# Loads cut in halves, and single row copies issued earlier, in a rank-ordered row scatter

## Chip, cores and metric

The kernel runs on one core of one Trainium2 chip. The metric is the device time of one execution in microseconds (us), as the median over several runs. The record gives every run in this document the state "fast" (granted TensorE clock 0.51 to 0.59). "Span" is the time from first to last instruction; in the recorded runs it is 1.7 to 2.0 us shorter than the device time. Every ratio compares a kernel with runs of the kernel before from the same rounds.

## The reference

Each of 8 batches has 2048 rows of 2560 float32 (10 KB a row). Row i goes to the place that its score takes in the sorted order of its batch:

```python
x = randn(8, 2048, 2560); scores = randn(8, 2048)
ranks = argsort(argsort(scores, axis=1), axis=1)
out[b, ranks[b, i], :] = x[b, i, :]
```

168 MB are read and 168 MB are written; the arithmetic is only the ranking.

## The kernel before

VectorE counts, for each score, how many scores of its batch are smaller. Rows then travel in two ways. All of them are moved by DMAs. The profile counts 16 DMA engines, which the queues share: from 200 to 240 us the packets of the three queues take 94.0, 4.2 and 4.2% of the time of 16 engines, 102% together. q0 is GpSimd's queue, q1 is SP's (SyncE) and q10 is ACT's (ScalarE). What was handed to a queue and has not yet passed is called its ring here; SP's and ACT's held up to 36 rows each. The trace records packets. A row copy is 16 packets of 640 B and 16 of 4 B (12,672 of each for ACT's 792 rows); loads and scatters come to 144 packets each (25,920 for 180 DMAs on q0), 128 of data (of 4 B for the 56 thin rows, which the scatters leave out) and 16 small ones. The small packets, 16 to a DMA, are called completion packets here.

The bulk of the rows goes through on-chip memory. GpSimd loads a block of 256 rows (2.6 MB, two rows to a partition) into one of 8 buffers and scatters it with two indirect DMAs of 128 rows each. It loads four blocks ahead, and a buffer is loaded again when its scatters have landed. The first 8 loads are made as two DMAs of 10 KB a partition, the other 50 as one of 20 KB:

```python
NBUF = 8; LAG = 4
BULK = [(b, g) for b in range(B) for g in range(len(GROUPS)) if g or b not in DIRECT]   # 58 blocks
HALVED = range(8)

def load(line, k, sem):
    ...
    for j in range(m if k in HALVED else 1):
        part = slice(j * D, (j + 1) * D) if k in HALVED else slice(0, m * D)
        line.eng.dma_start(out=xb[k % NBUF][:, part], in_=rows[:, part]).then_inc(sem, 16)
...
for k, (b, g) in enumerate(BULK):
    if k >= LAG and k + NBUF - LAG < len(BULK):
        scatters_done(pl, k - LAG)
        load_ahead(k + NBUF - LAG)
    pl.wait(*loaded[k])
    pl.after(dve, t_bulk[b, g])
    for j in range(GROUPS[g][1]):
        scatter(k, j)
nc.gpsimd.drain()
```

The other rows are copied one by one inside DRAM, by SP and ACT on queues of their own. The first block of batches 0 to 5 is copied in a hardware loop (128 rows on each of the two engines per batch), and seven further sets of 8 rows ("thin" rows) in straight-line code:

```python
todo = list(enumerate(THIN))                 # THIN = [(b, 4) for b in 1..7]
for b in DIRECT:                             # batches 0..5
    while todo and todo[0][1][0] < b:
        n, where = todo.pop(0)
        thin_rows(n, *where)                 # 8 rows, on SP or ACT in turn
    for h, (line, name) in enumerate(((sp, ENG.SP), (act, ENG.Activation))):
        line.after(dve, t_rows[b])
        with line.eng.Fori(0, half // G) as q:      # 16 rows a turn
            ...
for n, where in todo:
    thin_rows(n, *where)
for line in (sp, act):
    line.wait(s_rows[line], 16 * n_rows[line])
...
for k in range(max(0, len(BULK) - NBUF), len(BULK)):
    scatters_done(sp, k)
```

At the end SP waits for its row copies and for the last scatters. In the program the row wait stands first, but in the traces SP's step for it comes after the scatter waits (778.3 against 769.9 us in the kernel before).

Of the kernel before, what the change touches and what calls it, by code (L numbers as in the profile page):

```python
# [40 lines left out]
def kernel(  # L41
# [15 lines left out]
    DIRECT = range(6)  # L57
# [9 lines left out]
    THIN = [(b, 4) for b in range(1, B)]  # L67
    HOLES = range(48, 48 + 4)

    HALVED = range(8)  # L70

    STEPS = [(0, 1), (1, 2), (2, 4), (4, 8)]

# [28 lines left out]
    with tc.tile_critical(no_gpsimd_drain=True):  # L102
# [17 lines left out]
        def load(line, k, sem):  # L120
            b, g = BULK[k]
            r, m = GROUPS[g]
            rows = x[b, r:r + P * m, :].rearrange("(p j) d -> p (j d)", j=m)
            for j in range(m if k in HALVED else 1):
                part = slice(j * D, (j + 1) * D) if k in HALVED else slice(0, m * D)
                line.eng.dma_start(  # L126
                    out=xb[k % NBUF][:, part], in_=rows[:, part]
                ).then_inc(sem, 16)
                if k:
                    n_load[k % NBUF] += 1  # L130
# [3 lines left out]
        load(sp, 0, s_first)  # L134
        loaded = {0: (s_first, 16 * (2 if 0 in HALVED else 1))}

# [224 lines left out]
        def thin_rows(n, b, g):  # L361
            line, name = ((sp, ENG.SP), (act, ENG.Activation))[n % 2]
            r, m = GROUPS[g]
            line.after(dve, t_rows[b, g])
            _, at = nc.values_load_multi_w_load_instructions(
                thin_i[b, g][:],
                engines=[name],
                min_val=b * N * ROW,
                max_val=(b * N + N - 1) * ROW,
                skip_runtime_bounds_check_because=(  # L370
                    "a rank counts other scores of one batch of N, so it lies in 0..N-1"
                ),
            )
            for i in range(4 * m):
                row = b * N + r + HOLES[i % 4] * m + i // 4
                line.eng.dma_start(
                    out=out_bytes[bass.ds(at[i], ROW)],
                    in_=x_bytes[bass.ds(row * ROW, ROW)],
                ).then_inc(s_rows[line], 16)
                n_rows[line] += 1  # L380

        todo = list(enumerate(THIN))
        for b in DIRECT:
            while todo and todo[0][1][0] < b:
                n, where = todo.pop(0)
                thin_rows(n, *where)
            for h, (line, name) in enumerate(((sp, ENG.SP), (act, ENG.Activation))):
                line.after(dve, t_rows[b])
                half = WIDE // 2
                with line.eng.Fori(0, half // G) as q:  # L390
                    _, at = nc.values_load_multi_w_load_instructions(
                        rows_i[b][:, bass.ds(half * h + q * G, G)],
                        engines=[name],
                        min_val=b * N * ROW,
                        max_val=(b * N + N - 1) * ROW,
                        skip_runtime_bounds_check_because=(
                            "a rank counts other scores of one batch of N, so it lies in 0..N-1"
                        ),
                    )
                    for i in range(G):  # L400
                        row = b * N + GROUPS[0][0] + half * h + i
                        line.eng.dma_start(
                            out=out_bytes[bass.ds(at[i], ROW)],
                            in_=x_bytes[bass.ds(q * (G * ROW) + row * ROW, ROW)],
                        ).then_inc(s_rows[line], 16)
                n_rows[line] += half
# [73 lines left out]
```

## Time and profile before

| | before |
|---|---|
| device time | 782.2 us (782.14 to 783.19) |
| span of the profiled run (its device time 781.49 us) | 779.7 us |
| bulk: packets on q0 (data and completion) | 25,920 |
| row copies: SP (q1), ACT (q10) | 800 and 792 rows |
| last packet of q0 / of SP's rows / of ACT's rows | 769.4 / 775.4 / 773.3 us |

The prediction below shows the lines of this profile. In the slices of the span, a digit is the busy share of one fortieth of the span in tenths. In the DMA view, a queue has its packets, its megabytes and its share of the time of 16 engines. In the list of waits, an entry has the total, the number of times and the longest, in us. The last packets come from the trace's record of each DMA packet, which has start, duration, queue and size but not the engine.

### The profile page before, as it was taken

How to read it: one execution, taken by the hardware profiler on the slowest of the kernel's cores; microseconds unless marked ns; L12 is line 12 of the kernel's file. 1: busy time of each engine (PE TensorE's matmuls, PEld its weight loads, DVE VectorE, ACT ScalarE, POOL GpSimd, SP SyncE). 2: the span in 40 equal slices, each digit the busy share in tenths (PEclk: the TensorE clock that was granted, in tenths of full speed). 3: DMA queues.
4: the chain of work that ended last, by engine and by line, in shares of the span. 5: the costliest groups of instructions: out<-in, count | busy, mean ns of one | idle time of the engine just before them, and what ended most of it. 6: DMA issues, size and time to landing. Idle time of an engine off the chain costs nothing.

```text
span 779.7 us, 8177 instructions
## 1 busy us (share of the span) xinstructions
PE 35.4 (5%) x170; PEld 30.5 (4%) x170; DVE 399.8 (51%) x825; ACT 0.0 (0%) x1; POOL 150.2 (19%) x189
## 2 busy tenths in 40 slices
PE   4000020020020020120000000000000000000000
PEld 4000010010010010120000000000000000000000
DVE  5999979979979979899999200000000000000000
ACT  0000000000000000000000000000000000000000
POOL 4113122212121211112121212121212121220100
PEclk9999995555555555565555555555555555555555
DMA  8999999999999999999999999999999999999995
GB/s 360 418 419 419 426 415 425 415 421 416 424 418 424 416 421 417 425 417 423 419 421 420 422 419 421 420 422 422 417 425 416 426 416 425 417 424 418 419 415 101
DMA packets 77186, 320.15 MB, mean 411 GB/s; under 512 B 28448, under 2 KB 53920, under 8 KB 53920
## 3 DMA queue, kind: packets, MB, share of 16 engines
q0 software_dynamic: 25920, 300.90, 90.7%
q1 hardware_dynamic: 25904, 10.93, 5.5%
q10 hardware_dynamic: 25344, 8.16, 4.5%
q14 instruction: 17, 0.14, 0.0%
q8 instruction: 1, 0.02, 0.0%
HBM read 168.41 MB, written 168.35 MB: 432 GB/s over the span
## 4 chain that ended last, share of the span: by engine, by line
DMA 49%; another core or an unknown queue 19%; DVE 13%; POOL 7%; issue 6%; PE 1%; POOLq 0%; SPq 0%
DMA out_dram<-x,rank_i 43%; DVE trash L238 12%; DMA x<-in_x_dram 6%; POOL out_dram L422 5%; POOL x L126 1%; PE ps_all L196 0%; DVE s_all L339 0%; DMA s_in<-in_scores_dram 0%; PE ps_col L175 0%; POOLq L446 0%; DVE rank_i L276 0%; DVE rank L270 0%; DVE rank L264 0%; PE ps_row L298 0%
## 5 line engine op out<-in xcount | busy, mean ns | idle before, releaser
L238 DVE TENSOR_SCALAR_CACHE_REDUCE trash<-s_all,s_col 128x1792 bf16<-128x1792 f32 (+7 forms) x240 | 315.2, 1348 | 4.6
L422 POOL DMA_INDIRECT out_dram<-x,rank_i x116 | 112.7, 972 | 141.8 <-DMA x<-in_x_dram 36.4
L126 POOL DMA_DIRECT2D x<-in_x_dram x64 | 35.7, 560 | 445.7 <-DMA out_dram<-x,rank_i 426.6
L238 DVE SCALAR_TENSOR_TENSOR trash<-s_all,s_col,mask 128x256 bf16<-128x256 f32 x128 | 61.6, 481 | 0.0
L196 PE MATMUL ps_all<-ident,s_col 128*128 128x128 f32 x128 | 28.5, 416 | 3.1 <-DVE s_all L339 2.8
L196 PEld LDWEIGHTS ps_all<-ident,s_col 128*128 128x128 f32 x128 | 26.8, 226 | 4.2 <-DVE s_all L339 3.2
L298 PE MATMUL ps_row<-ident,rank 128*1 128x128 f32 x26 | 7.0, 366 | 392.5 <-DVE rank_i L284 335.2
L339 DVE COPY s_all<-ps_all 128x512 f32<-128x512 f32 x32 | 20.2, 685 | 1.7 <-PE ps_all L196 1.4
L238 DVE DVE_READ_ACCUMULATOR trash<-s_all,s_col 128x1 f32 x240 | 19.9, 83 | 0.0
L298 PEld LDWEIGHTS ps_row<-ident,rank 128*1 128x1 f32 x26 | 1.9, 95 | 395.8 <-DVE rank_i L284 337.6
L238 DVE DVE_READ_ACCUMULATOR trash<-s_all,s_col,mask 128x1 f32 x128 | 10.6, 83 | 0.0
L309 DVE TENSOR_SCALAR thin_i<-ps_row 1x8 int32<-1x8 f32 x7 | 1.1, 154 | 17.7 <-PE ps_row L298 17.7
L324 DVE TENSOR_SCALAR rows_i<-ps_row 1x256 int32<-1x256 f32 x6 | 2.5, 412 | 4.1 <-PE ps_row L298 4.1
L183 DVE COPY s_col<-ps_col 128x128 f32<-128x128 f32 x1 | 0.3, 290 | 4.5 <-PE ps_col L175 4.5
L175 PE MATMUL ps_col<-ident,s_in 8*128 8x8 f32 x16 | 2.1, 262 | 3.6 <-DMA s_in<-in_scores_dram 3.6
L175 PEld LDWEIGHTS ps_col<-ident,s_in 8*128 8x128 f32 x16 | 2.0, 211 | 3.6 <-DMA s_in<-in_scores_dram 3.6
L276 DVE CAST rank_i<-rank 128x16 int32<-128x16 f32 (+3 forms) x11 | 1.9, 173 | 0.4
L270 DVE TENSOR_TENSOR rank<-rank,acc 128x16 f32<-128x16 f32 (+3 forms) x11 | 1.9, 170 | 0.4
L264 DVE TENSOR_TENSOR rank<-acc,acc 128x16 f32<-128x16 f32 (+3 forms) x11 | 1.9, 170 | 0.4
L284 DVE TENSOR_SCALAR rank_i<-rank,hole 128x2 int32<-128x2 f32 x7 | 1.6, 228 | 0.2
L156 POOL TENSOR_SCALAR_AFFINE_SELECT mask<-mask 128x256 f32<-128x256 f32 x2 | 0.8, 398 | 0.0
L168 DVE MEMSET acc<- 128x128 f32 x1 | 0.2, 165 | 1.1 <-SPq L102 1.1
(10 smaller groups left out, 1.8 us busy)
## 6 DMA issues: line engine op xcount, KB each, us to landing
x<-in_x_dram POOLq DMA_DIRECT2D x50, 2560.0 KB
x<-in_x_dram POOLq DMA_DIRECT2D x14, 1280.0 KB
out_dram<-in_x_dram SPq DMA_DIRECT2D x800, 10.0 KB
out_dram<-in_x_dram ACTq DMA_DIRECT2D x792, 10.0 KB
x<-in_x_dram SPq DMA_DIRECT2D x2, 1280.0 KB, 9.3
out_dram<-x,rank_i POOLq DMA_INDIRECT x116, 48.4
s_in<-in_scores_dram SPq DMA_DIRECT2D x1, 64.0 KB
```

Source lines behind the costliest of these rows:

```text
L126: line.eng.dma_start(out=xb[k % NBUF][:, part], in_=rows[:, part]).then_inc(sem, 16)
L175: nc.tensor.transpose(out=ps_col[:, B * c:B * (c + 1)], in_=s_in[:, r + j:r + m * P:m], identity=ident[:B, :B],)
L196: nc.tensor.transpose(out=ps_all[:, P * c:P * (c + 1)], in_=s_col[:, c, b:b + 1].to_broadcast([P, P]), identity=ident[:],)
L238: do(out=trash[i][:, :P * (hi_c - lo_c)], in0=s_all[:, P * lo_c:P * hi_c], accum_out=acc[i][:, col:col + 1], **how,)
L264: nc.vector.tensor_tensor(out=rank[:, cols], in0=acc[0][:, cols], in1=acc[1][:, cols], op=OP.add)
L270: nc.vector.tensor_tensor(out=rank[:, cols], in0=rank[:, cols], in1=acc[2][:, cols], op=OP.add)
L276: nc.vector.tensor_copy(out=rank_i[:, cols], in_=rank[:, cols])
L284: nc.vector.tensor_scalar(out=rank_i[:, cols], in0=rank[:, cols], scalar1=hole[:], scalar2=None, op0=OP.add,)
L298: nc.tensor.transpose(out=ps_row[:1, P * j:P * (j + 1)], in_=rank[:, col:col + 1], identity=ident[:],)
L324: nc.vector.tensor_scalar(out=rows_i[b][:].rearrange("o (p j) -> o p j", p=P), in0=ps_row[:1, :WIDE].rearrange("o (j p) -> o p j", p=P), s ...
L339: nc.vector.tensor_copy(out=s_all[:, 512 * q:512 * (q + 1)], in_=ps_all[:, 512 * q:512 * (q + 1)],)
L422: nc.gpsimd.indirect_dma_start(out=out_flat, out_offset=bass.IndirectOffsetOnAxis(ap=rank_i[:, col:col + 1], axis=0), in_=xb[k % NBUF][:, ...
```

## The change

Two things are altered: 12 more loads are issued as halves, and the thin rows of batches 5 to 7 are issued ahead of the last loop in place of after it. The intent is to let the row copies keep pace, so that they don't end after everything else.

```diff
-    HALVED = range(8)
+    HALVED = range(20)
@@
-            while todo and todo[0][1][0] < b:
+            while todo and (todo[0][1][0] < b or b == DIRECT[-1]):
```

## The prediction

> **What bounds the kernel now.** I read the slices of the span first, because the kernel only moves rows: 300.90 MB go through the chip's memory (load, then scatter) and about 16 MB are copied row by row inside DRAM.
>
> ```profile
> POOL 4113122212121211112121212121212121220100
> DMA  8999999999999999999999999999999999999995
> DMA packets 77186, 320.15 MB, mean 411 GB/s; under 512 B 28448, under 2 KB 53920, under 8 KB 53920
> q0 software_dynamic: 25920, 300.90, 90.7%
> q1 hardware_dynamic: 25904, 10.93, 5.5%
> q10 hardware_dynamic: 25344, 8.16, 4.5%
> ```
>
> The 16 DMA engines are at 90% or more in 38 of 40 slices. GpSimd, which issues the loads and scatters, is busy 19%, VectorE stops at two thirds of the span. So neither issuing nor ranking sets the end; the bytes do, and only the two ends of the span hold slack. q0 is GpSimd's queue; q1 and q10 belong to SP and ACT, which copy single 10 KB rows as 16 pieces of 640 B.
>
> Next I read the DMA view of a steady stretch (200 to 240 us; columns: packets, MB, share of 16 engines):
>
> ```profile
> q0 software_dynamic: 1311, 16.02, 94.0%
> q1 hardware_dynamic: 1307, 0.42, 4.2%
> q10 hardware_dynamic: 1309, 0.42, 4.2%
> ```
>
> The three queues move **the same number of packets**, whatever a packet's size. One completion packet follows each data packet of a row copy, so two turns are one sixteenth of a row. A row queue therefore advances in proportion to the number, not the bytes, of q0's packets.
>
> Last I read SP's waits (us in total, times, longest) and the four-microsecond windows of the tail (start:end, length, five engines, clock, DMA share, GB/s):
>
> ```profile
> SPq L102 <- DMA out_dram<-in_x_dram: 8.3, 1, 8.3
> ...
> 764.00:768.00 4.00, 0.00 (x0) 0.00 (x0) 0.00 (x0) 0.00 (x0) 0.00 (x0) 0.50 1.06 109
> 768.00:772.00 4.00, 0.00 (x0) 0.00 (x0) 0.00 (x0) 0.00 (x0) 0.00 (x0) 0.50 0.59 38
> 772.00:776.00 4.00, 0.00 (x0) 0.00 (x0) 0.00 (x0) 0.00 (x0) 0.00 (x0) 0.50 0.09 5
> ```
>
> SP saw the last scatter land at 769.9 us and then waited until 778.3 for its row copies. In that time the engines move 109, 38 and 5 GB/s in place of some 420. **The row queues end last**, q0 has already run dry, and small packets alone do not fill the engines: a 640 B packet takes 32 ns in the steady state, but 95 to 233 ns on average (by window and queue) from 764 to 772 us.
>
> [...] The packet records show it: 386 ns for 10 KB, 762 ns for 20 KB, so splitting costs 2 x 386 - 762 = 10 ns.
>
> **The change, part by part.**
>
> 1. Halves. Loads 8 to 19 (12 of 58) become two DMAs. On q0 that adds 12 x 128 / 16 = 96 data packets and 12 completion packets per engine. The direct cost is 96 x 10 ns + 12 x 9 ns, about 1.1 us per engine. It lies on the path, since the engines are the bound.
> GpSimd gets 12 more issues at 563 ns (the row of the loads): 6.8 us spread over some 160 us where it is idle most of the time, 426.6 us of the whole run waiting for scatters. No cost at the end.
>
> 2. What the halves do to the row queues. The whole loads start to appear on q0 at about 81 us; at some 13 us a load (50 of them from 81 to 736 us), loads 8 to 19 cover about 81 to 238 us. There q0's average packet falls from (395 x 762 + 768 x 387 + 153 x 9) / 1316 = 456 ns (my count of a 40 us window) to about 350 ns. With two row turns of about 20 ns each, and the overlap of 1.02, a round falls from 0.49 to 0.38 us, so a row could pass each queue every 0.76 us in place of 0.97. But SP and ACT issue no faster than 0.74 us a row plus about 1.6 us for each 16 rows of the loop, and measured 40 to 48 rows in 40 us (0.83 to 1.0 us a row). So in this stretch the row queues become **limited by issue**, and their backlog does not build up.
> How much that is: in the kernel before, the time from issuing a row to its last packet grows from about 5 us at 60 us to about 17 us at 240 us. With halves I expect it to stay near 6 us. The saving of about 10 us at one row per 0.9 us is 11 rows per queue, up to 15 by the other count (176 issued against 160 to 162 passed from 80 to 240 us). After that both kernels go one to one again, the ring fills to about 32 rows (the most outstanding in the trace), and the lead of 11 to 15 rows stays to the end. So not all 48 rows which 96 extra packets could carry per queue are gained.
>
> 3. The tail. When q0 runs dry engine by engine (about 764 us on average), some 30 rows of SP and 18 of ACT are left (row packets after 764 us, 393 and 199, over 16, are 25 and 12[...]). A lead of 22 to 30 rows leaves 18 to 26. The engines pass about 22 rows in 4 us there (360 packets from 764 to 768 us, over 16), so 22 to 30 fewer rows end 4 to 5.5 us sooner; q0's end moves back by the cost of the halves (1.1 us) and by those rows, which now lie before it: 26 x 41 ns (32 of data, 9 of completion) = 1.1 us. Net: 4.7 - 2.2 = **2.5 us less**, with up to 1.5 us more if the last packets, which trickle at 5 GB/s from 772 us, vanish rather than shift.
>
> 4. Single row copies ahead of the last loop. No DMA is added or removed. SP's 16 and ACT's 8 last thin rows (batches 5 to 7) move from after 752 us to about 620 us, when their ranks have long been ready (VectorE ends before 460 us). Straight code issues a row per 0.63 us, the loop one per about 0.84 us, but about 30 rows are outstanding at 740 us, so the engines do not run out. [...] I take 0, plus or minus 0.5 us.
>
> Sum: -2.5 -0.75 (half of the 1.5) = about **-3.3 us**. 782.2 - 3.3 = 778.9 us.
>
> **Rivals.** (a) *The transfers merely trade places.* The engines are full, splitting adds 1.1 us, and if issue stalls keep the row queues from gaining, the time is 782 to 783. For it: from 40 to 80 us, where q0 has only 10 KB packets, SP issues only 40 rows in 40 us. Against it: from 160 to 280 us it issues 45 to 48. (b) *The tail closes fully.* Rows end before q0, and SP then ends on the scatters: 769.9 + 2.2 = 772.1 in place of 778.3, 6.2 us less, so 776. For it: with one-to-one turns, 108 further q0 turns would carry up to 54 rows per queue, more than are left. Against it: the issue limit. (c) *q0 starves.* The row queues take more turns while loads wait for scatters, and GpSimd becomes the bound; 785 or more. Against it: q0's scatters land 47 us after issue, so its backlog is deep, and GpSimd issues its last scatter at 737.6, 32 us before it lands.
>
> **Range and chances.** The range runs from a closed tail with some help by the moved rows (774.5) to no effect with noise (782.5). A 2% gain needs 15.6 us. From 764 us to SP's release at 778.3 there are only 14.3 us, and some 2 us of engine work is still to do in them, so it is out of reach; a 2% loss would need q0 to run dry in mid-span.
>
> **What would show it.** Right: q0 has 1,536 more 10 KB packets and 12 x 16 more completion packets; row packets from 80 to 240 us rise from about 5,150 to some 5,500 per row queue; SP's last wait for row copies shrinks from 8.3 to about 2 to 5 us; its last scatter is seen 1.5 to 2.5 us later; the 768 to 772 window is fuller or the span ends sooner. Wrong in the mechanism: the row packets in that stretch do not rise. Wrong in size: the row copies end before the scatters (then 776), or the moved rows leave issue gaps at the end. Wrong altogether: a slice of the DMA row under 9 in mid-span.

Three readings in part 3 are estimates, as the records don't carry the engine: that q0 runs dry engine by engine (its share falls from 74.6% at 760 to 764 us to 12.7% and 1.3% in the next two windows), the mean of 764 us, and the 30 and 18 rows then left, of which the trace shows 25 and 12 as packets after 764 us.

## More of the kernel before

GpSimd has a drain instruction after its last scatter, which in the traces ends 1.7 to 5.2 us after q0's last packet (4.3 us in the kernel before). Then comes the end barrier: in the kernel before, the next steps of the other engines start at 778.49 to 778.50 us, right after SP's at 778.45.

## The result

The changed kernel takes **778.83 us** (778.41 to 780.5, 4 runs) against 782.21 us before (4 runs), ratio 0.9958 with a 95% interval of 0.9941 to 0.9975. A ratio here is the mean time of one kernel's fast runs over the mean of the other's fast runs of the same rounds, so not quite the ratio of the quoted medians. The result is correct.

First the slices and the queues of the changed kernel:

```profile
DMA  8999999999999999999999999999999999999995
DMA packets 78914, 320.15 MB, mean 412 GB/s; under 512 B 28640, under 2 KB 54112, under 8 KB 54112
q0 software_dynamic: 27648, 300.90, 91.2%
```

The bytes are the same. q0 has 1,728 packets more, which is 12 x 128 data and 12 x 16 completion packets: 3,072 packets of 10 KB stand in place of 1,536 of 20 KB. The engines are still at 90% or more in 38 of 40 slices.

The DMA view of 80 to 240 us, where loads 8 to 19 go by, first the kernel before:

```profile
q0 software_dynamic: 5268, 63.87, 93.9%
q10 hardware_dynamic: 5181, 1.67, 4.2%
q1 hardware_dynamic: 5131, 1.65, 4.1%
```

and the changed kernel:

```profile
q0 software_dynamic: 6929, 63.03, 93.5%
q10 hardware_dynamic: 5496, 1.77, 4.5%
q1 hardware_dynamic: 5482, 1.77, 4.4%
```

A row is 16 data and 16 completion packets. SP's queue passed (5482 - 5131) / 32 = **11 rows more** in the stretch, ACT's (5496 - 5181) / 32 = 10. q0 passed 0.84 MB less. (Counted from the start of the span the lead at 240 us is 11 and 8 rows, since ACT had passed 64 packets fewer by 80 us.) The row queues no longer match q0 packet for packet here (6,929 on q0): SP and ACT issue too slowly to use every turn. In these 160 us they issued 175 and 176 rows and passed 171 and 172, so that little was left standing (about 6 rows on each at 240 us). The time from the issue of a row to its last packet is about 6 us on both for rows issued from 230 to 240 us, against 18 us (SP) and 17 us (ACT) in the kernel before; at 60 us, before any backlog, it is 5 us in both kernels.

SP's waits at the end of the changed kernel:

```profile
SPq L28 <- DMA out_dram<-x,rank_i: 13.2, 4, 4.0
SPq L102 <- DMA out_dram<-in_x_dram: 3.8, 1, 3.8
```

The wait for row copies has fallen from 8.3 to 3.8 us. The last scatter is seen at 772.1 us in place of 769.9, the last row copy at 775.9 in place of 778.3.

The windows of the tail (start:end, length, five engines, clock, DMA share, GB/s):

```profile
764.00:768.00 4.00, 0.00 (x0) 0.00 (x0) 0.00 (x0) 0.00 (x0) 0.00 (x0) 0.50 1.04 238
768.00:772.00 4.00, 0.00 (x0) 0.00 (x0) 0.00 (x0) 0.00 (x0) 0.00 (x0) 0.50 0.18 43
772.00:776.00 4.00, 0.00 (x0) 0.00 (x0) 0.00 (x0) 0.00 (x0) 0.00 (x0) 0.50 0.02 1
```

The window from 764 us moves 238 GB/s in place of 109: q0 lasts longer into it (to 771.2 us in place of 769.4), and fewer small packets follow (from 764 us on 495 row pieces in place of 592).

One thing shows here that I had not reckoned with. GpSimd's drain after its last scatter ends at **776.33 us**, 0.4 us after SP has seen its last row. In the kernel before it ended at 773.6 us, hidden behind the row copies (778.3). The drain's own step, first before and then in the changed kernel (duration in ns, start in us):

```profile
L446 POOLq DRAIN  x1: 37464/37464/37464, 736.1 to 736.1; - x1
L446 POOLq DRAIN  x1: 37234/37234/37234, 739.1 to 739.1; - x1
```

The changed kernel ends on two waits that are nearly level, and in this profile the drain is the later one.

### The profile page after: what moved, and what is told of

It is laid out like the page before. It is cut to its first block, busy times and chain, and to the rows that moved or that the text cites. A ratio compares the mean times of both kernels' runs of the same rounds, so it can differ in the third digit from the quotient of the medians.

```text
span 777.4 us, 8189 instructions
## 1 busy us (share of the span) xinstructions
PE 34.6 (4%) x170; PEld 29.9 (4%) x170; DVE 400.0 (51%) x825; ACT 0.0 (0%) x1; POOL 157.4 (20%) x201
## 4 chain that ended last, share of the span: by engine, by line
DMA 44%; DVE 36%; another core or an unknown queue 5%; issue 4%; PE 3%; POOL 3%; POOLq 0%; SPq 0%
DMA out_dram<-x,rank_i 38%; DVE trash L238 34%; DMA x<-in_x_dram 6%; PE ps_all L196 2%; POOL out_dram L422 2%; DVE s_all L339 2%; POOL x L126 1%; PE ps_row L298 0%; DMA s_in<-in_scores_dram 0%; PE ps_col L175 0%; DVE rank L270 0%; DVE rank_i L276 0%; DVE rank L264 0%; POOLq L446 0%
## 5 line engine op out<-in xcount | busy, mean ns | idle before, releaser
L126 POOL DMA_DIRECT2D x<-in_x_dram x76 | 42.6, 563 | 441.8 <-DMA out_dram<-x,rank_i 411.1
```

## The experiments

Eleven kernels ran, each with 5 rounds beside the kernel before; all gave the correct result. Runs a to d shared their runs of the kernel before (median 781.77 us), as did e to h (782.55 us) and j to l (782.32 us).

The theory, drawn from the equal packet counts of the three queues (1311, 1307 and 1309 from 200 to 240 us): the queues take turns packet by packet, so more and smaller q0 packets give the row queues more turns. The row copies then end earlier, until something else holds the end. The rivals: the new order of the row copies did it; halves help the loads as such; only their number counts.

### a_halves_only and b_order_only: each part alone

```diff
a:  HALVED = range(20), the row copies in the order of before
b:  HALVED = range(8),  the row copies in the new order
```

> Only the halves of the change; the single row copies stay behind the last loop. Theory (the row queues get a turn per q0 packet, so more and smaller q0 packets let the row copies end sooner): the whole effect of the change, ratio to before 0.996 (0.9945 to 0.9975), SP's last wait for row copies about 4 us in place of 8.3, row packets per row queue from 80 to 240 us about 5,480. Rival (the order of the row copies did it): ratio 1.000, wait 8 us.

> Only the new order of the row copies; 8 loads in halves as before. Theory: ratio 1.000 (0.9985 to 1.001), SP's last wait for row copies 7.5 to 9 us. Rival (the order did it): ratio 0.996, wait about 4 us.

Measured: a 777.86 us, ratio 0.9948 (0.9935 to 0.9962); b 782.01 us, ratio 1.0003 (0.9989 to 1.0016). SP's wait for row copies in a:

```profile
SPq L102 <- DMA out_dram<-in_x_dram: 3.6, 1, 3.6
```

and in b:

```profile
SPq L102 <- DMA out_dram<-in_x_dram: 8.8, 1, 8.8
```

The halves are the whole effect; the new order does nothing that can be seen. The rival "order" falls. That a is a shade faster than the whole change isn't shown: their intervals, from different rounds, overlap. The row packets of a from 80 to 240 us are 5,644 and 5,663, more than the 5,480 expected; its queues had passed 143 and 125 fewer before 80 us, where it is the same as the kernel before, and the lead at 240 us counted from the start is 12 and 11 rows.

### c_late_halves: the same number of halves, in another place

```diff
-    HALVED = range(20)
+    HALVED = [*range(8), *range(46, 58)]
```

> As many halved loads as in the changed kernel (20), but loads 8 to 19 are whole and loads 46 to 57 halved. Theory: in that late stretch some 32 rows stand in each ring, so the extra turns are all used, up to some 40 rows per queue in place of 11 to 15; the row copies then end before the scatters, SP ends on the scatters, 776 to 777 us (ratio 0.993), last scatter at about 773 us in the span, wait for row copies 0 to 2 us. Rival (only the number of halved loads counts, or halves help the loads themselves at the start): 778.9 us, wait 3.8 us as in the changed kernel, or no gain.

Measured: 777.87 us, ratio 0.9951 (0.9938 to 0.9965). The expected mechanism came, the expected time didn't. The DMA view from 580 to 740 us, first the kernel before:

```profile
q0 software_dynamic: 5315, 63.83, 93.6%
q1 hardware_dynamic: 5318, 1.71, 4.3%
q10 hardware_dynamic: 5316, 1.71, 4.3%
```

then this run:

```profile
q0 software_dynamic: 6863, 62.40, 92.1%
q10 hardware_dynamic: 6672, 2.15, 5.4%
q1 hardware_dynamic: 6613, 2.13, 5.3%
```

SP's queue passed (6613 - 5318) / 32 = 40 rows more, ACT's 42: four times the lead that early halves give, as expected. Here some 30 rows stand in each ring to use the turns (32 on each at 600 us in the kernel before), while from 80 to 240 us SP and ACT could not issue fast enough. So for the row copies the place counts, not only the number: they ended at 760 us (SP) and 747 us (ACT), ten us and more before the last scatter (seen at 770.6 us). The times alone would not show it, since a took 777.86 us with the same number of halves. The span of c ended only at 775.7 us. SP's waits say why:

```profile
SPq L28 <- DMA out_dram<-x,rank_i: 14.4, 5, 3.0
SPq L102 <- POOLq L102: 3.8, 1, 3.8
```

SP waits 3.8 us for GpSimd's queue. GpSimd's drain ended at 774.8 us, 4.7 us after q0's last packet. Closing the gap of the row copies uncovered **a third wait**.

### d_halves_32: more halves from the start

```diff
-    HALVED = range(20)
+    HALVED = range(32)
```

> The changed kernel with 32 in place of 20 loads in halves. Theory: the backlog of the row queues stays small until about 395 us, the lead grows to about 27 rows per queue, the row copies end with the scatters or before them, 776 to 777.5 us (ratio 0.993), wait for row copies 0 to 2 us, last scatter at about 773 us. Rival (the tail is already as short as it gets and each further half costs 0.1 us): 780 us.

Measured: **774.96 us** (774.85 to 775.1), ratio 0.9912 (0.9898 to 0.9925), better than I expected. By 395 us the lead is 28 rows on SP and 31 on ACT, near the 27 expected. SP's waits:

```profile
SPq L28 <- DMA out_dram<-x,rank_i: 29.6, 8, 8.3
SPq L390 <- DVE rows_i L324: 15.5, 1, 15.5
SPq L102 <- POOLq L102: 0.9, 1, 0.9
```

No wait for row copies is left; they end at 766.7 us (SP) and 756.1 us (ACT). The last scatter is seen at 771.0 us. The drain ended at 772.35 us, only 1.7 us after q0's last packet, so that 3 us less than in c were spent on it. My expectation had no drain in it: the last scatter came 2 us sooner than I had put, and the drain's short lag is why that showed in the time.

### g_late_no_drain and h_32_no_drain: the drain taken away

```diff
-        nc.gpsimd.drain()
```

in c and in d. SP still waits for every scatter and row copy, so the output is complete.

> The late halves (20 loads: 0 to 7 and 46 to 57) without GpSimd's drain after its last scatter; SP still waits for every scatter and every row copy. In the late-halves run the row copies had ended by 760 us and SP had seen the last scatter at 770.6 us, but GpSimd's drain ended at 774.8 us and held the end. Theory (the drain is the new last wait): ratio to before falls from 0.9951 to about 0.991 to 0.992, GpSimd's step of the end barrier comes right after SP's at about 771, span about 772.5. Rival (the drain only waits for something that the end barrier waits for as well): ratio stays 0.995.

> 32 loads in halves without the drain. In the run with the drain its end came only 1.3 us after SP had seen the last scatter, in place of some 4. Theory: about 1 us less than with it, 773.5 to 775 us, ratio 0.990 to 0.991. Rival (drain is free here): ratio 0.991, the same as with it.

Measured: g 782.22 us, ratio 0.9995 (0.9981 to 1.0009); h 776.26 us, ratio 0.9918 (0.9905 to 0.9932). My theory failed in g: the drain was the last wait, but taking it away gained nothing, and the time is also above what the rival foretold (0.995). GpSimd's first step of the end barrier did come at 770.39 us in g, right after SP's. But the end of the program contains a drain of its own, and it now took 8.4 us (770.47 to 778.87) in g and 2.7 us in h. SP's waits in g:

```profile
SPq L28 <- DMA out_dram<-x,rank_i: 23.2, 8, 4.0
SPq L474 <- PEq L474: 8.7, 2, 8.3
```

The view names PE, but the records of the end show every engine but GpSimd ready by 771 us: this is a case where the named engine had long been done. So a drain holds the end in both kernels, this one in c and the program's own in g. Begun at 741.9 us, beside the last scatters, it ended 4.7 us after q0's last packet (c); begun after them, 9.2 us after (g). For 32 halves the two are 1.7 and 3.4 us in the profiles; the gain that I foretold for h didn't come, and the ratios of d and h overlap. With the late halves the drain is clearly better begun early (0.9951 against 0.9995). What GpSimd still has to do in it, the records don't show.

### e_halves_all and f_halves_none: the two ends of the scale

```diff
e:  HALVED = range(58)
f:  HALVED = range(0)
```

> All 58 loads in halves, drain kept. Theory: SP and ACT are limited by issue all through (a row per 0.87 us), so the row copies end at about 725 us, some 45 us ahead of the scatters; each further half beyond what balances the tail costs its packets: 26 loads x 8 x 10 ns and 26 completions x 9 ns, 2.3 us more than with 32, and q0 alone at the end loses some of the overlap of 1.02 (1 us). So 777 to 779 us, ratio 0.995 (0.993 to 0.997). Rival (halved loads are better in themselves): below 775 us, ratio under 0.991.

> No load in halves, new order of row copies. Theory: in the first 80 us the row queues get a turn per 20 KB packet of the loads, fall behind at once, and some 10 rows per queue more than before are left when q0 runs dry: ratio 1.005 (1.002 to 1.008), SP's last wait for row copies 11 to 14 us. Rival (the first 8 halves do nothing for the end, only for the start): ratio 1.000, wait 8 to 9 us.

Measured: e 777.25 us, ratio 0.993 (0.9917 to 0.9944); f 784.17 us, ratio 1.0018 (1.0005 to 1.0032). In e the row copies ended at 740.4 us (SP) and 708.4 us (ACT); the last scatter was seen at 772.0 us and the drain ended at 774.7 us. The time lies in the range that I expected, but partly by luck. Against d, q0's last packet is 1.0 us later, where I had put 2.3 us and 1 us for lost overlap; the other 1.3 us are the drain's longer lag (3.0 us in place of 1.7), which I had not put at all. Halves beyond what lets the row copies end with the scatters bring nothing more here, and they cost less on q0 than I had put: 50 more halves than before moved the last scatter from 769.9 to 772.0 us, although the records of q0's data packets sum to 3.35 us more per engine (708.85 against 705.50) and the row copies lie before it as well.

In f SP's rows ended 3 us later than before (778.3 against 775.4), but the slowdown was a third of what I expected. SP's wait:

```profile
SPq L102 <- DMA out_dram<-in_x_dram: 9.0, 1, 9.0
```

Before 80 us the row queues passed 95 (SP) and 139 (ACT) row pieces of 640 B fewer than in the kernel before, 6 and 9 rows, not 10 on each. Even that is not clean: the other kernels, whose first 8 loads are all halved alike, vary by 90 and 82 pieces in the same stretch, and the kernel before stands at the top of that. From 80 to 160 us f's queues passed 4 (SP) and 3 (ACT) rows more than in the kernel before, as a standing backlog would let them. The wait of 9.0 us understates the delay, as SP was still issuing rows until 771 us. The rival (no effect of the first halves on the end) is excluded by f's interval, though narrowly. But f also has the new order, and the interval of b, its nearest control, reaches 1.0016 and overlaps with f's; so the small effect of the first halves is likely and not fully shown.

### j_halves_26, k_halves_40 and l_32_old_order: what the drain follows, and the order again

```diff
j:  HALVED = range(26)
k:  HALVED = range(40)
l:  HALVED = range(32), row copies in the order of before
```

> 26 loads in halves, new order, drain kept. The row copies should end within 1 us of the last scatter (some 771 us), so GpSimd's drain holds the end. It came 4.3 to 5.1 us after q0's last packet in every run with 173 to 192 DMAs on q0, and 1.7 and 3.0 us after it with 204 and 230. Reading 1 (what is left for the drain follows the number of DMAs like a sawtooth that has fallen by 204): with 198 it is either still about 5 us (776 span, ratio 0.995) or already about 1.5 us (773 span, ratio 0.991). Reading 2 (the drain is late only where row copies run beside it to the end, and early where they have ended): about 5 us.

> 40 loads in halves, new order, drain kept: 212 DMAs on q0. Row copies end well ahead of the scatters (about 755 us). Reading 1: drain about 2.1 us after q0's last packet, between the 1.7 of 32 and the 3.0 of 58 halves; span 774, ratio 0.992. Reading 2 and the cost of halves alone: the drain 1.7 us after, ratio 0.9917.

> 32 loads in halves, row copies in the old order. Theory (the order does nothing, also where the tail is closed): ratio 0.991 as with the new order (0.9898 to 0.9925), row copies end 3 to 10 us before the last scatter. Rival (the new order matters once the row queues no longer end last): slower by 0.2% or more.

Measured: j 778.17 us, ratio 0.9948 (0.9934 to 0.9961); k 775.76 us, ratio 0.9918 (0.9904 to 0.9931); l 774.95 us, ratio 0.9909 (0.9896 to 0.9923).

l is as fast as d, with the same drain: the order does nothing to the time with a closed tail either. (SP's row copies ended at 769.5 us, 1.5 us before the last scatter was seen, nearer than the 3 to 10 us that I expected.) j and k extend the drain's row. Here is every kernel that kept its drain, by the number of DMAs on q0 (116 scatters, and the loads, less the first one, which SP issues):

| loads in halves | DMAs on q0 | q0's last packet, us | drain ends, us | lag, us | SP sees last row copy, us |
|---|---|---|---|---|---|
| 0 (f) | 173 | 769.6 | 774.0 | 4.4 | 781.3 |
| 8 (before; b) | 180 | 769.4; 769.7 | 773.6; 774.3 | 4.3; 4.7 | 778.3; 779.5 |
| 20 (after; a; c, late) | 192 | 771.2; 770.5; 770.1 | 776.3; 775.3; 774.8 | 5.1; 4.7; 4.7 | 775.9; 774.7; at once |
| 26 (j) | 198 | 770.2 | 775.4 | 5.2 | 771.9 |
| 32 (d; l) | 204 | 770.7; 770.7 | 772.4; 772.4 | 1.7; 1.7 | at once |
| 40 (k) | 212 | 770.9 | 772.9 | 2.0 | at once |
| 58 (e) | 230 | 771.7 | 774.7 | 3.0 | at once |

"At once" means that the row copies had landed before SP came to that wait, after the last scatter. The lag rises slowly with the number (by 0.8 us from 173 to 198, where kernels of the same number differ by 0.4), falls by 3.5 us between 198 and 204, and rises again. The device times agree with the fall: j's five runs took 777.97 to 778.49 us and k's 775.58 to 776.07 us in the same rounds. Reading 1 (it follows the number, like a sawtooth) foresaw 2.1 us for k and 2.0 came; it allowed either outcome for j, so j doesn't test it. Reading 2 (it follows whether row copies run to the end) falls by c, where they had ended ten us earlier and the lag was 4.7 us, and by l, where SP's ran to within 1.2 us of q0's last packet and the lag was 1.7 us. Why the lag follows the number isn't shown: the runs vary DMAs and packets together, and one profile per kernel is a thin base. It is **open**.

The table also settles the rival that halves help the loads as such: in each of its kernels with more halves than before, q0's last packet is 0.7 to 2.3 us later than the 769.4 us of the kernel before, never earlier.

j against l, from the same rounds, is the cleanest lesson: six more halved loads take 3.2 us off the time. The drain ends 3.0 us sooner, and the row copies were the last wait in neither kernel.

## Why the prediction was right

**What bounds the kernel.** Right: the row queues ended last. Every kernel with its first 26 loads or fewer halved and no others shows SP waiting for row copies after the last scatter; with 32 (d) that wait is gone and the time is shorter. Two readings on the way were wrong and changed nothing: VectorE stops at 435 us, 56% of the span and not two thirds, and a recount of rows issued but not yet passed gives up to 36, not 32.

**The turns.** Right. The queues pass one recorded packet a turn: 1311, 1307 and 1309 in 40 us. If each DMA were one turn, the 144 packets of a load against the 32 of a row would give counts of 9 to 2 to 2. In c, 12 halved loads where a backlog stands gave the row queues nearly a turn for each extra q0 packet (1,548 more on q0, 1,295 and 1,356 more on the row queues).

**The issue limit.** Right, and it set the size: a lead of 11 and 10 rows in the changed kernel where 11 to 15 were foretold, 40 and 42 in c where the limit doesn't hold. The named sign, some 5,500 row packets per queue from 80 to 240 us, came as 5,482 and 5,496. Another sign was miscounted: "1,536 more 10 KB packets" should be 1,536 more data packets in all, 3,072 more of 10 KB for 1,536 fewer of 20 KB.

**The tail.** Right in mechanism and nearly in size. From q0's last packet to SP's last row packet there are 6.0 us before and 1.8 us after, so the shorter queue is worth 4.2 us where 4.7 were foretold; q0's last packet comes 1.9 us later where 2.2 were foretold. The difference, 2.4 us by which SP's last row packet comes sooner, stands against the foretold 2.5. The further 0.75 us, half of an "up to 1.5", is seen nowhere by itself. The two profiled runs differ by 2.4 us of device time (781.49 and 779.13), the medians by 3.4, and the interval of the ratio allows 2.0 to 4.6 us. That 778.9 was foretold and 778.83 came is therefore good fortune in the last microsecond.

The working behind the tail was coarser than the process. I used the mean rate of all engines (22 rows in 4 us). In the kernel before, the last four completions of SP's row pieces land 0.19 to 0.20 us apart, and ACT's last four 0.36 to 0.39 us apart. The 4.2 us would be 22 pieces of 0.19 us; why the last pieces come at that pace is not shown. From SP's last row packet until SP saw its rows done it took 2.9 us in both kernels, so this step did not change.

**The cost on q0.** Its last scatter came 2.2 us later in the profile of the change, as foretold, but 1.1 us later in a and 0.7 us in c, where many more row copies were ahead of it. The term is rather too large. e says the same of the halves. (These are single profiles.)

**The order of the row copies.** Right at 0 (b, and l against d).

**The rivals.** (a) fell: the interval of the ratio excludes 1. (c) fell: no slice in mid-span is under 9. (b) did not come either, as SP still waited 3.8 us for its row copies, and a step was missing in it: "SP then ends on the scatters" left out GpSimd's drain. In c the row copies ended well ahead of the scatters, and the time was 777.9 us, not 776, because the drain ended 4.7 us after q0's last packet. In the changed kernel itself the drain (776.33 us) already comes level with the row copies (775.93 us), so the foretold time was met with one of its two last waits unnamed. That the drain ended only 0.4 us after the row copies, and not later, is luck.

**A faster version.** With 32 halves (d, l) the kernel takes 774.95 us, 0.9% less than before and also below the changed kernel, because there the row copies end before the scatters and the drain's lag is low. The prediction's rival (b), a closed tail, put the same end at 776 us.

## What to carry to other kernels

Where several queues share full DMA engines, count packets as well as bytes. The queues of small packets went forward in step with the number of packets of the large one (1307 and 1309 against 1311), and cutting the large ones shifted the share at about 10 ns a cut (2 x 386 against 762 ns), provided that the small queue had work standing ready (40 and 42 rows gained in c, 11 and 10 where it had not). Try to let all queues run dry together; cuts beyond that brought nothing here (774.96 us with 32 halves, 777.25 us with 58). Before you forecast what a closed gap is worth, list every wait that ends the program and when each one ends now, the hidden ones too; here, in the kernel before, the drain ended 4.7 us and the last scatter 8.4 us before the row copies.
